# Norms as one power of a sum: means, signs and scales folded into factors, epsilon added on another engine

## The chip, the cores and the metric

The kernel runs on one core of a Trainium2 chip, as one launch. The metric is the device time of that launch in microseconds (us); smaller is better. The engines are called PE (TensorE matmul; its weight loads are listed apart as PEld), DVE (VectorE), ACT (ScalarE), POOL (GpSimd) and SP (SyncE, which here issues DMAs).

## What is computed

Two layers of a decoder, 256 positions, width 1024, all float32. Each layer normalises x, projects it through one combined matrix, runs three groups of attention heads (MoBA with one block of 256, which at this length is plain causal attention; differential attention; DSA, which keeps the 64 keys that an indexer scores highest), projects their outputs back and adds a SwiGLU feed-forward layer.

```python
def rms_norm(x, g):
    y = x * rsqrt(mean(x * x, axis=-1, keepdims=True) + EPS)     # EPS = 1e-6
    return y * g
for l in range(2):
    h = rms_norm(x, attn_norm_g[l])
    (mq, mk, mv, dq, dk, dv, sq, sk, sv, iq, ik, iw) = split(h @ w_in[l])
    def qk(t, nh, g):                       # heads of 64
        return apply_rope(rms_norm(split_heads(t, nh), g), cos, sin)
    moba = attention(qk(mq, 4, qg[0]), qk(mk, 4, kg[0]), mv)
    dq_h, dk_h = qk(dq, 8, qg[1]), qk(dk, 8, kg[1])
    lam = exp(sum(lp[0] * lp[1])) - exp(sum(lp[2] * lp[3])) + lam_init
    diff = (softmax(q1 k1) - lam * softmax(q2 k2)) @ dv
    diff = rms_norm(diff, diff_subln_g[l]) * (1.0 - lam_init)
    score = sum_h(iw * relu(rope(iq) . rope(ik)))      # -inf above the diagonal
    keep  = the min(256, S / 4) keys of highest score
    dsa  = attention(qk(sq, 4, qg[2]), qk(sk, 4, kg[2]), sv, keep)
    x = x + concat(moba, diff, dsa) @ w_out[l]
    h2 = rms_norm(x, ffn_norm_g[l])
    x = x + (silu(h2 @ w_gate[l]) * (h2 @ w_up[l])) @ w_down[l]
```

## The kernel before

**Products.** Every product with a weight matrix is taken in three matmuls that add up in one bank (L618, L619, L620): the weight's rounded part `wh` times the activation's rounded part `hH`, the weight's rest `wl` times `hH`, and `wh` times the activation's rest `hL`. For each loaded weight `raw`, ACT writes `wh` as a copy (L252) and DVE writes `wl` as a subtraction (L541). The positions are two tiles of 128 (`t` = 0, 1). The layer's first part is called the mixers here: the projection in eight chunks of columns, `idx` (the indexer), `sv_iq`, `mqk`, `dq`, `dk`, `sqk`, `mv`, `dv`, with the heads' work in between, then the output projection.

**Who sets the order.** All work is written as Python threads that hand pieces to a planner (`Timeline`). A piece is `V`, `A`, `G` or `T` (DVE, ACT, POOL, PE) with an estimated cost, and a thread can wait for an event or for a buffer. The planner keeps an estimated clock for each engine, takes the piece that can start first, and issues instructions in that order; on the chip each engine then works strictly in that order. So a changed cost or a piece moved to another engine reorders the program around it. DMAs of weights are issued from SP's queue in the order of the loads; `SMALL_FIRST` says ahead of which load the small ones go: the rope angles, the gains of queries and keys (`gqk`), the causal penalties (`pens`, 256 KB), and others.

**The norms.** A reciprocal root is taken on POOL by `rsqrt_mean` (L621): one `tensor_scalar` that multiplies the sum of squares by 1/n and adds epsilon (L626), then a power of -0.5 (L629). There are three kinds.

- Over the width of 1024 (`rx_thread`, L723): ACT squares two halves of a row (L714), POOL adds the two sums (L726), and `rsqrt_mean` gives `rx`. Ahead of the mixers POOL then works out an epsilon for the heads' norms (L733, L735), since the heads are normed from projections that were not scaled by `rx`.
- Over the 64 numbers of a head (`head_rstd`, L806): ACT squares a 128x512 tile (L819), DVE sums it by heads (L823), and `rsqrt_mean` gives eight factors for each position: `dkr` for the keys of the differential heads, `rq` for the others, the queries among them. Another POOL instruction (L833) multiplies the factors of queries by -(64^-0.5). In `qk_thread` (L851) DVE multiplies the roped keys by their factors (L879; in some places ACT does, L871), PE transposes them (L636), and the scores' matmuls (L1037) follow. The queries' factors go into the softmax as a scale for each position (L1007).
- Over the 128 numbers of a differential output head (`diff_out`, L1160): ACT sums squares (L1183), `rsqrt_mean`, DVE multiplies (L1192), PE transposes (L636), and DVE multiplies by the gain (L1204).

**Tables.** `table_thread` (L1377) multiplies the rope angles by the gains of queries and keys, 12 POOL instructions in each layer (L1386, L1391), into the table `tb` that the rope of the next heads reads (L778, L790). `gcol_thread` (L1314) transposes the gains of the width's norms into columns. `lambda_thread` (L1339) loads 256 KB into a work buffer `w` (L1346) and works out lambda on DVE (L1359, L1370). The indexer's scores are picked by rounds of MAX (L986) and MATCH_REPLACE (L987), then turned into penalties (L991, L994).

## Time and profile before

| | |
|---|---|
| median of 3 runs | 650.46 us (648.71 to 650.91) |
| the profiled execution | 650.43 us, of which the span from first to last instruction is 648.4 us |
| PE busy | 633.2 us, 98% of the span |
| DVE busy | 554.8 us, 86% |
| ACT busy | 411.7 us, 63% |
| POOL busy | 84.2 us, 13% |
| granted TensorE clock | 0.999 of full speed on average |

The shares are means over unlike stages. The projections and feed-forward products keep PE full; in the mixers, and above all in the first 90 us, DVE has as little spare time as PE, and POOL's short norms lie between DVE and PE. The 2.0 us between the execution's time and its span lie outside of every engine's work.

### The profile page before, as it was taken

How to read it: one execution, taken by the hardware profiler on the slowest of the kernel's cores; microseconds unless marked ns; L12 is line 12 of the kernel's file. 1: busy time of each engine (PE TensorE's matmuls, PEld its weight loads, DVE VectorE, ACT ScalarE, POOL GpSimd, SP SyncE). 2: the span in 40 equal slices, each digit the busy share in tenths (PEclk: the TensorE clock that was granted, in tenths of full speed). 3: DMA queues.
4: the chain of work that ended last, by engine and by line, in shares of the span. 5: the costliest groups of instructions: out<-in, count | busy, mean ns of one | idle time of the engine just before them, and what ended most of it. 6: DMA issues, size and time to landing. Idle time of an engine off the chain costs nothing.

```text
span 648.4 us, 8749 instructions
## 1 busy us (share of the span) xinstructions
PE 633.2 (98%) x3132; PEld 515.5 (79%) x3132; DVE 554.8 (86%) x924; ACT 411.7 (63%) x733; POOL 84.2 (13%) x119
## 2 busy tenths in 40 slices
PE   9899999999999999999999999999999999999997
PEld 8777877787788888787889788887777888888886
DVE  5789999566999999999488999995599999999861
ACT  6487779647647566556545688894677385565640
POOL 2414340200000000180020333200100000000000
PEclk9999999999999999999999999999999999999999
DMA  8898343607558467328736145343475566670621
GB/s 246 284 307 220 111 151 127 199 2 265 188 183 271 142 187 253 132 66 286 246 122 213 60 131 195 130 151 110 145 245 167 188 230 195 192 252 11 215 110 65
DMA packets 74350, 113.36 MB, mean 175 GB/s; under 512 B 2722, under 2 KB 54724, under 8 KB 74308
## 3 DMA queue, kind: packets, MB, share of 16 engines
q1 hardware_dynamic: 73700, 110.71, 52.5%
q0 software_dynamic: 576, 2.10, 1.8%
q8 instruction: 24, 0.39, 0.3%
q14 instruction: 18, 0.15, 0.1%
q10 hardware_dynamic: 32, 0.01, 0.0%
HBM read 109.66 MB, written 1.05 MB: 171 GB/s over the span
## 4 chain that ended last, share of the span: by engine, by line
PE 70%; DVE 18%; DMA 5%; ACT 4%; issue 1%; POOL 1%; SPq 0%; DVEq 0%; POOLq 0%; ACTq 0%
PE bank L618 21%; PE bank L620 21%; PE bank L619 21%; DVE wl L541 7%; PE bank L636 4%; DMA raw<-in_w_in_dram 2%; DMA raw<-in_w_up_dram 2%; PE bank L1037 1%; DMA w<-in_diff_lambda_dram 1%; ACT p L1018 1%; ACT wh L252 1%; DVE qr L550 1%; DVE tb L976 1%; DVE tb L987 1%; ACT p L254 1%
## 5 line engine op out<-in xcount | busy, mean ns | idle before, releaser
L252 ACT ACTIVATE wh<-raw 128x1024 fp32r<-128x1024 f32 (+4 forms) x205 | 207.7, 1039 | 99.6 <-PE bank L620 48.3
L541 DVE TENSOR_TENSOR wl<-raw,wh 128x1024 fp32r<-128x1024 f32 (+4 forms) x205 | 245.4, 1206 | 24.6 <-ACT wh L252 23.9
L618 PE MATMUL bank<-wh,hH 128*128 128x512 f32 (+3 forms) x488 | 191.4, 392 | 2.5 <-ACT hH L252 2.3
L619 PE MATMUL bank<-wl,hH 128*128 128x512 f32 (+3 forms) x488 | 185.3, 380 | 2.0 <-DVE wl L541 1.9
L620 PE MATMUL bank<-wh,hL 128*128 128x512 f32 (+3 forms) x488 | 185.4, 380 | 0.7 <-DVE hL L668 0.5
L618 PEld LDWEIGHTS bank<-wh,hH 128*128 128x128 f32 x488 | 91.9, 188 | 22.6 <-issue 4.5
L620 PEld LDWEIGHTS bank<-wh,hL 128*128 128x128 f32 x488 | 91.8, 188 | 18.3 <-DVE hL L668 2.0
L619 PEld LDWEIGHTS bank<-wl,hH 128*128 128x128 f32 x488 | 92.0, 189 | 17.9 <-DVE wl L541 3.5
L618 PE MATMUL bank<-wh,qk 128*128 128x512 f32 x176 | 70.3, 400 | 0.0
L620 PE MATMUL bank<-wh,qk 128*128 128x512 f32 x176 | 69.7, 396 | 0.6 <-DVE qk L1246 0.6
L619 PE MATMUL bank<-wl,qk 128*128 128x512 f32 x176 | 69.6, 395 | 0.0
L252 ACT ACTIVATE qk<-bank 128x512 fp32r<-128x512 f32 (+4 forms) x54 | 26.1, 501 | 29.7 <-PE bank L636 29.0
L620 PEld LDWEIGHTS bank<-wh,qk 128*128 128x128 f32 x176 | 33.2, 189 | 9.2 <-DVE qk L1246 1.5
L618 PEld LDWEIGHTS bank<-wh,qk 128*128 128x128 f32 x176 | 33.2, 188 | 7.6 <-ACT qk L252 0.4
L619 PEld LDWEIGHTS bank<-wl,qk 128*128 128x128 f32 x176 | 33.2, 189 | 7.4
L618 PE MATMUL bank<-wh,pv 128*128 128x512 f32 x96 | 38.0, 395 | 0.0
L619 PE MATMUL bank<-wl,pv 128*128 128x512 f32 x96 | 37.9, 395 | 0.0
L620 PE MATMUL bank<-wh,pv 128*128 128x512 f32 x96 | 37.9, 395 | 0.0
L1018 ACT ACTIVATE p<-p,small 128x128 f32<-128x128 f32 (+1 forms) x64 | 28.6, 451 | 3.7 <-DVE small L1007 3.6
L757 DVE TENSOR_TENSOR x<-x,bank 128x512 f32<-128x512 f32 x16 | 11.0, 686 | 22.0 <-PE bank L620 22.0
L618 PE MATMUL bank<-wh,mH 128*128 128x512 f32 x64 | 26.1, 407 | 0.0
L636 PE MATMUL bank<-ident,p 128*128 128x128 f32 x160 | 25.0, 275 | 0.9 <-DVE p L1226 0.6
(147 smaller groups left out, 905.1 us busy)
## 6 DMA issues: line engine op xcount, KB each, us to landing
raw<-in_w_in_dram SPq DMA_DIRECT2D x22, 1024.0 KB, 5.2
raw<-in_w_down_dram SPq DMA_DIRECT2D x22, 1024.0 KB, 5.0
raw<-in_w_gate_dram SPq DMA_DIRECT2D x32, 512.0 KB, 4.1
raw<-in_w_up_dram SPq DMA_DIRECT2D x32, 512.0 KB, 5.0
raw<-in_w_out_dram SPq DMA_DIRECT2D x8, 1024.0 KB, 4.8
raw<-in_w_in_dram SPq DMA_DIRECT2D x4, 768.0 KB, 7.0
wl<-raw POOLq DMA_DIRECT2D x4, 512.0 KB, 7.1
tb<-in_w_gate_dram SPq DMA_DIRECT2D x4, 512.0 KB, 5.5
```

The lines of the kernel that those rows point to most:

```text
L252: nc.scalar.activation(dst, src, AF.Copy)
L254: nc.scalar.activation(dst, src, AF.Copy, scale=scale)
L541: lambda: nc.vector.tensor_sub(lo[:, cs], raw[:, cs], h[:, cs].bitcast(F32)),
L550: return V(n, lambda: nc.vector.tensor_tensor(dst, a, b, op=op))
L618: nc.tensor.matmul(o, aH[:, kt, tok], wH[:, k, cols], start=start, stop=False)
L619: nc.tensor.matmul(o, aH[:, kt, tok], wL[:, k, cols], start=False, stop=False)
L620: nc.tensor.matmul(o, aL[:, kt, tok], wH[:, k, cols], start=False, stop=stop)
L636: nc.tensor.transpose(o, i, ident)
L757: e = yield V(512, lambda: nc.vector.tensor_add(xt[t][:, cs], xt[t][:, cs], bank))
L976: lambda: nc.vector.scalar_tensor_tensor(sc, rl[:, i * n : (i + 1) * n], iws[t][:, h : h + 1], prev, op0=OP.mult, op1=OP.add,),
L987: end = yield V(n, lambda: nc.vector.match_replace(sc, m8, sc, NEG_IDX))
L1018: lambda: nc.scalar.activation(p[:, spans[t]], p[:, spans[t]], AF.Exp, bias=mn[:, t : t + 1], scale=-1.0, accum_out=se[t],),
```

## The change

The factors of the norms are redefined so that a reciprocal root is one POOL instruction, the power of a sum.

- `rsqrt_mean` becomes `rsqrt`: the power alone, without the multiplication by 1/n. What is missing is put elsewhere: the width's gains `gcol` are multiplied by the root of 1024 as they are copied (DVE), the gains of the differential outputs by a root of 128/1024 more, the keys' gains by the root of 64, and the queries' gains by -1, once, on POOL ahead of layer 0's tables.
- The queries' factors are then right without L833. Since their sign moves, the penalties in `pens` that the indexer uses are multiplied by -1 (POOL, once), and the indexer's own by a sign in L991.
- Epsilon is added by itself. For the width, POOL adds it to the first half's sum of squares as soon as that is there. For the heads DVE adds it (the new L827, `small<-small,ss 128x8`), 16 times in the kernel. For the differential outputs POOL adds it, in the place of L626.
- The heads' epsilon takes one POOL instruction in place of two.
- `pens` is loaded ahead of one more weight, and the tables wait for it.

```diff
-SMALL_FIRST = {5: "ropes", 6: "gqk", 8: "pens", 10: "late"}
+SMALL_FIRST = {5: "ropes", 6: "gqk", 7: "pens", 10: "late"}
...
-    def rsqrt_mean(dst, ssum, n, inv, eps=EPS):
-
-        yield G(170, lambda: nc.gpsimd.tensor_scalar(dst, ssum, inv, eps, op0=OP.mult, op1=OP.add))
-        return (
-            yield G(
-                290 + 166 * n, lambda: nc.gpsimd.tensor_tensor(dst, dst, nhalf[:, :n], op=OP.pow)
-            )
+    def rsqrt(dst, src, n):
+
+        return G(
+            290 + 166 * n, lambda: nc.gpsimd.tensor_tensor(dst, src, nhalf[:, :n], op=OP.pow)
         )
...
-        yield ("wait", both)
         s = ss2[t]
+        yield ("wait", halves[0])
+        yield G(170, lambda: nc.gpsimd.tensor_scalar_add(s[:, 0:1], s[:, 0:1], D * EPS))
+        yield ("wait", halves[1])
         yield G(170, lambda: nc.gpsimd.tensor_add(s[:, 0:1], s[:, 0:1], s[:, 1:2]))
-        e = yield from rsqrt_mean(rx[t], s[:, 0:1], 1, 1.0 / D)
+        e = yield rsqrt(rx[t], s[:, 0:1], 1)
         ready.done(e)
         if mixers:
 
-            yield G(
+            e = yield G(
                 170,
-                lambda: nc.gpsimd.tensor_scalar(s[:, 1:2], s[:, 0:1], 1.0 / D, EPS, op0=OP.mult, op1=OP.add),
+                lambda: nc.gpsimd.tensor_scalar_mul(s[:, 1:2], s[:, 0:1], HD * EPS),
             )
-            e = yield G(170, lambda: nc.gpsimd.tensor_scalar_mul(s[:, 1:2], s[:, 1:2], EPS))
...
         yield ("wait", eps_ready[t])
-        e = yield from rsqrt_mean(dst, small[:, :n], n, 1.0 / HD, ss2[t][:, 1:2])
+        yield V(
+            n, lambda: nc.vector.tensor_scalar_add(small[:, :n], small[:, :n], ss2[t][:, 1:2]), ap=1
+        )
+        e = yield rsqrt(dst, small[:, :n], n)
         SMALL.put(small, e)
         done["rstd"].done(e)
-        nq = done["queries"]
-        if nq:
-            e = yield G(
-                200, lambda: nc.gpsimd.tensor_scalar_mul(dst[:, :nq], dst[:, :nq], -(HD ** -0.5))
-            )
-        done["all"].done(e)
...
-            lambda: nc.vector.tensor_scalar(sc, sc, -1.0e38, NEG, op0=OP.is_gt, op1=OP.mult),
+            lambda: nc.vector.tensor_scalar(sc, sc, -1.0e38, -NEG, op0=OP.is_gt, op1=OP.mult),
...
-        yield from rsqrt_mean(ro[:, :4], ro[:, :4], 4, 1.0 / P)
+        yield G(170, lambda: nc.gpsimd.tensor_scalar_add(ro[:, :4], ro[:, :4], P * EPS))
+        yield rsqrt(ro[:, :4], ro[:, :4], 4)
...
-        e = yield V(n, lambda: nc.vector.tensor_copy(gcol[:, c0 : c0 + n], bank[:, :n]))
+        e = yield V(
+            n, lambda: nc.vector.tensor_scalar_mul(gcol[:, c0 : c0 + n], bank[:, :n], D ** 0.5)
+        )
...
-                        gcol[:, c : c + 1], gcol[:, c : c + 1], 1.0 - lam_init(l)
+                        gcol[:, c : c + 1], gcol[:, c : c + 1],
+                        (1.0 - lam_init(l)) * (P / D) ** 0.5,
...
         yield ("wait", small_in["ropes"])
+        yield ("wait", small_in["pens"])
         yield ("wait", small_in["gqk"])
+        if l == 0:
+
+            for s, factor in enumerate((-1.0, HD ** 0.5)):
+                yield G(500, lambda: nc.gpsimd.tensor_scalar_mul(gqk[:, s], gqk[:, s], factor))
+            yield G(
+                300, lambda: nc.gpsimd.tensor_scalar_mul(pens[:, 0, P:], pens[:, 0, P:], -1.0)
+            )
```

Counted over the program, POOL loses 30 rows (115 to 85), DVE gains 17 (852 to 869: 16 are the new adds; three more of the copies that make `wh` also fall to DVE instead of ACT), and PE and SP keep theirs, in another order. The lines of the changed file are a few lower than before's for the same statement (L879 is L874 there, L823 is L822, L636 is L633).

On DVE, in the mixers of layer 0 where the keys of the differential heads (chunk `dk`) are normed, the rows of before are these; `small_129` and `small_130` are the sums of squares of the two tiles, `dkr_85_162` the factors.

```order
L823 TENSOR_REDUCE small_129<-w_26_101 128x8
L778 TENSOR_TENSOR qr_105<-bank_67,tb_159 128x512
L823 TENSOR_REDUCE small_130<-w_28_103 128x8
L790 TENSOR_TENSOR w_29_104<-bank_67,tb_159 128x512
L541 TENSOR_TENSOR wl_100<-raw_90,wh_99 128x1024
L550 TENSOR_TENSOR qr_105<-qr_105,w_29_104 128x512
L541 TENSOR_TENSOR wl_100<-raw_90,wh_99 128x1024
L987 MATCH_REPLACE tb_159<-small_118,tb_159 128x256
L879 TENSOR_TENSOR qr_105<-qr_105,dkr_85_162 128x512
```

The same place of the changed kernel, from the rope's product behind the first sum on (L822 stands in front of it):

```order
L777 TENSOR_TENSOR qr_105<-bank_69,tb_159 128x512
L827 TENSOR_SCALAR small_129<-small_129,ss_71_146 128x8
L789 TENSOR_TENSOR w_26_101<-bank_69,tb_159 128x512
L822 TENSOR_REDUCE small_130<-w_28_103 128x8
L541 TENSOR_TENSOR wl_100<-raw_90,wh_99 128x1024
L550 TENSOR_TENSOR qr_105<-qr_105,w_26_101 128x512
L541 TENSOR_TENSOR wl_100<-raw_90,wh_99 128x1024
L827 TENSOR_SCALAR small_130<-small_130,ss_72_147 128x8
L541 TENSOR_TENSOR wl_94<-raw_91,wh_93 128x1024
L777 TENSOR_TENSOR qr_106<-bank_68,tb_159 128x512
L822 TENSOR_REDUCE small_131<-w_27_102 128x8
L874 TENSOR_TENSOR qr_105<-qr_105,dkr_85_162 128x512
```

The second tile's sum now passes through an add that stands behind two weight subtractions and a rope's addition, and the multiply of the keys behind one more subtraction, a rope's product and a sum.

On PE, where the second tile's keys of chunk `mqk` are transposed in layer 0 (`qr_107`), before has the four transposes behind the last of four trios of matmuls into one bank:

```order
L618 MATMUL bank_67<-wh_97,hH_139 128x512
L619 MATMUL bank_67<-wl_98,hH_139 128x512
L620 MATMUL bank_67<-wh_97,hL_140 128x512
L636 MATMUL bank_64<-ident_73,qr_107 128x128 x4
L618 MATMUL bank_68<-wh_97,hH_139 128x512
```

The changed kernel has them behind the first of the four (the bank is `bank_65` there):

```order
L620 MATMUL bank_66<-wh_95,hL_140 128x512
L618 MATMUL bank_65<-wh_97,hH_139 128x512
L619 MATMUL bank_65<-wl_98,hH_139 128x512
L620 MATMUL bank_65<-wh_97,hL_140 128x512
L633 MATMUL bank_69<-ident_73,qr_107 128x128 x4
```

They stand three trios, nine matmuls, earlier among the products.

On SP's queue, early in the program, the penalties move ahead of one load of a weight and lambda's input behind two (`raw` are weights, `w_28_103` receives lambda's input):

```order
 L350 DMA raw_90<-in_w_in_dram 128x4x384
+L1296 DMA pens_83<-in_causal_dram 128x2x256
 L350 DMA raw_91<-in_w_in_dram 128x4x512
-L1300 DMA pens_83<-in_causal_dram 128x2x256
 L350 DMA raw_92<-in_w_in_dram 128x4x512
```

```order
 L350 DMA raw_92<-in_w_in_dram 128x4x512
-L1346 DMA w_28_103<-in_diff_lambda_dram 128x512
 L350 DMA raw_90<-in_w_in_dram 128x4x512
 L350 DMA raw_91<-in_w_in_dram 128x4x512
+L1345 DMA w_28_103<-in_diff_lambda_dram 128x512
```

The rows with - are before's, those with + the changed kernel's: the penalties are issued one weight earlier, lambda's input two weights later.

## Rows read from the trace of the kernel before

**Rows 1.** The page: busy time of each engine; the chain that ended last.

```profile
PE 633.2 (98%) x3132; PEld 515.5 (79%) x3132; DVE 554.8 (86%) x924; ACT 411.7 (63%) x733; POOL 84.2 (13%) x119
...
PE 70%; DVE 18%; DMA 5%; ACT 4%; issue 1%; POOL 1%; SPq 0%; DVEq 0%; POOLq 0%; ACTq 0%
```

**Rows 2.** Windows, two stretches of the mixers (us, then busy us of each engine).

```profile
56.00:85.00 29.00, 27.68 (x141) 22.21 (x141) 27.77 (x79) 21.06 (x52) 11.15 (x10) 1.00 0.52 158
...
365.00:396.00 31.00, 31.00 (x162) 25.26 (x162) 30.80 (x81) 23.91 (x53) 11.77 (x13) 1.00 0.33 104
```

**Rows 3.** Timeline from 73 us, around layer 0's `dk` keys (start, us, engine).

```profile
78.48 1.67 POOL L629 TENSOR_TENSOR dkr<-dkr,nhalf 128x8 f32<-128x8 f32 x1
...
78.55 0.67 DVE L823 TENSOR_REDUCE small<-w 128x8 f32<-128x512 f32 x1
...
79.73 1.21 DVE L541 TENSOR_TENSOR wl<-raw,wh 128x1024 fp32r<-128x1024 f32 x1
...
80.25 1.35 POOL L626 TENSOR_SCALAR dkr<-small,ss 128x8 f32<-128x8 f32 x1
...
81.47 1.22 DVE L541 TENSOR_TENSOR wl<-raw,wh 128x1024 fp32r<-128x1024 f32 x1
...
81.69 2.49 POOL L629 TENSOR_TENSOR dkr<-dkr,nhalf 128x8 f32<-128x8 f32 x1
...
84.21 0.69 DVE L879 TENSOR_TENSOR qr<-qr,dkr 128x512 f32<-128x512 f32 x1 [1.13 <-POOL dkr L629]
...
84.96 1.09 PE L636 MATMUL bank<-ident,qr 128*128 128x128 f32 x8 [1.32 <-DVE qr L879]
```

**Rows 4.** Timeline from 54 us, the second tile's `mqk` keys in layer 0.

```profile
55.35 0.39 PE L620 MATMUL bank<-wh,hL 128*128 128x512 f32 x1
...
55.49 0.40 DVE L879 TENSOR_TENSOR qr<-qr,rq 128x256 f32<-128x256 f32 x1
55.58 0.80 PE L636 MATMUL bank<-ident,qr 128*128 128x128 f32 x4
```

**Rows 5.** Instructions by line and shape on DVE (busy us, mean ns, idle before).

```profile
L541 DVE TENSOR_TENSOR wl<-raw,wh 128x1024 fp32r<-128x1024 f32 x194 | 236.0, 1225 | 24.3 <-ACT wh L252 23.8
...
L1143 DVE TENSOR_SCALAR small<-small,nlam 128x2 f32<-128x2 f32 x8 | 1.8, 222 | 0.0
...
L896 DVE TENSOR_SCALAR iw<-bank,rx 128x8 f32<-128x8 f32 x4 | 1.1, 279 | 1.0 <-PE bank L620 1.0
```

**Rows 6.** Timeline, DVE alone, 86 to 106 us: two penalty instructions.

```profile
86.35 0.28 DVE L991 TENSOR_SCALAR tb<-tb 128x256 f32<-128x256 f32 x1
...
95.18 0.41 DVE L994 TENSOR_TENSOR tb<-tb,pens 128x256 f32<-128x256 f32 x1
```

**Rows 7.** Instructions by line, DVE, 273.4 to 288.6 us (POOL at layer 1's tables).

```profile
L541 DVE TENSOR_TENSOR wl<-raw,wh 128x1024 fp32r<-128x1024 f32 x4 | 5.8, 1462 | 0.0
```

**Rows 8.** Waits of DVE, 24 to 60 us (us in total, times, longest).

```profile
DVE wl L541 <- ACT wh L252: 2.4, 2, 1.7
```

**Rows 9.** Timeline, SP alone, 15 to 48 us: issues of penalties and weights.

```profile
15.55 1.27 SPq L1300 DMA_DIRECT2D pens<-in_causal_dram  x1
...
37.36 3.49 SPq L350 DMA_DIRECT2D raw<-in_w_in_dram  x2
```

**Rows 10.** DMA issues, 10 to 48 us: the penalties (KB, us to landing).

```profile
pens<-in_causal_dram SPq DMA_DIRECT2D x1, 256.0 KB, 11.1
```

**Rows 11.** Chain of waits, 30 to 48 us, around lambda (start, us, what).

```profile
34.66 6.44 DMA w<-in_diff_lambda_dram
```

**Rows 12.** Timeline, DVE alone, 40 to 48 us: lambda's first, the table's first reader.

```profile
41.12 0.23 DVE L1359 CUSTOM_DVE_ANT_0 w<-w 128x64 f32<-128x64 f32 x1 [0.67 <-DMA w<-in_diff_lambda_dram]
...
44.06 0.69 DVE L778 TENSOR_TENSOR qr<-bank,tb 128x512 f32<-128x512 f32 x1
```

**Rows 13.** Waits of PE, 114 to 150 us: the end of layer 0's mixers.

```profile
PE bank L636 <- DVE qr L1192: 1.0, 2, 0.7
```

**Rows 14.** Timeline, POOL alone, 146 to 151 us: the second norm.

```profile
146.75 0.19 POOL L726 TENSOR_TENSOR ss<-ss 128x1 f32<-128x1 f32 x1 [8.44 <-ACT w L714]
147.03 0.19 POOL L626 TENSOR_SCALAR rx<-ss 128x1 f32<-128x1 f32 x1
```

More of the change, by code (lines that the diff above doesn't have):

```diff
@@ L721, in square_thread, with rx_thread @@
         both.done(e)
-    def rx_thread(t, both, ready, mixers):
-        yield ("wait", both)
+    def rx_thread(t, halves, ready, mixers):
         s = ss2[t]
+        yield ("wait", halves[0])
+        yield G(170, lambda: nc.gpsimd.tensor_scalar_add(s[:, 0:1], s[:, 0:1], D * EPS))
+        yield ("wait", halves[1])
         yield G(170, lambda: nc.gpsimd.tensor_add(s[:, 0:1], s[:, 0:1], s[:, 1:2]))
-        e = yield from rsqrt_mean(rx[t], s[:, 0:1], 1, 1.0 / D)
+        e = yield rsqrt(rx[t], s[:, 0:1], 1)
         ready.done(e)
         if mixers:
-            yield G(
+            e = yield G(
                 170,
-                lambda: nc.gpsimd.tensor_scalar(s[:, 1:2], s[:, 0:1], 1.0 / D, EPS, op0=OP.mult, op1=OP.add),
+                lambda: nc.gpsimd.tensor_scalar_mul(s[:, 1:2], s[:, 0:1], HD * EPS),
             )
-            e = yield G(170, lambda: nc.gpsimd.tensor_scalar_mul(s[:, 1:2], s[:, 1:2], EPS))
             eps_ready[t].done(e)
@@ L744, in norm @@
         for t in range(NT):
-            both = Event(2)
+            halves = [Event(), Event()]
             for hf in range(2):
@@ L748, in norm @@
                 tl.spawn(norm_thread(t, hf, g0, h_ready[t][hf], r, kept), 0)
-                tl.spawn(square_thread(t, hf, None if kept else h_ready[t][hf], both), 1)
-            tl.spawn(rx_thread(t, both, r_ready[t], not kept), 1)
+                tl.spawn(square_thread(t, hf, None if kept else h_ready[t][hf], halves[hf]), 1)
+            tl.spawn(rx_thread(t, halves, r_ready[t], not kept), 1)
         return h_ready, r_ready
@@ L854, in qk_thread @@
         b = heads(bank)
-        nq = sum(p[1] for p in parts if not p[3])
-        ev = {"read": Event(), "rstd": Event(), "all": Event(), "queries": nq}
+        ev = {"read": Event(), "rstd": Event()}
         tl.spawn(head_rstd(bank, b, 8, t, rstd, ev), 10, full.time)
@@ L884, in qk_thread @@
         done.done(own.time)
-        yield ("wait", ev["all"])
-        r_done.done(ev["all"].time)
+        yield ("wait", ev["rstd"])
+        r_done.done(ev["rstd"].time)
     def idx_thread(t, bank, full, r_ready, done):
```

## The prediction

> **What bounds the kernel now.** The page comes first: PE is busy 633.2 of 648.4 us, and the chain that ended last runs through PE for 70% of the span, through DVE for 18% and through POOL for 1% [rows 1]. So nearly all of the time is products that the change leaves alone, and the change can act only where PE waits for an operand that passes through a norm. The windows tell where that is. In layer 0's mixers from 56 to 85 us PE is busy 27.68 of 29.00 us and DVE 27.77, so both are nearly full and PE's idle time is 1.3 us; in the like stretch of layer 1 PE is busy 31.00 of 31.00 [rows 2]. In layer 1 nothing can be won there, and only DVE's lateness could show.
>
> The 1.3 us is one wait, and the timeline shows its chain [rows 3]. DVE ends the second tile's sum of squares behind 78.55; POOL, still in the first tile's power, takes the epsilon at 80.25 (1.35 us, beside DVE's work) and the power at 81.69 (2.49 us); DVE's multiply of the keys starts at 84.21 after 1.13 us of waiting, and PE's eight transposes at 84.96 after 1.32 us. Two more waits of this kind, 1.0 us in all, stand at the end of layer 0's mixers behind the differential norm [rows 13]. POOL's short steps are on the path there, and in the second norm of the width, where L626 adds 147.03 - 146.75 = 0.28 us by the step from start to start [rows 14].
>
> **The change part by part.** I follow how late PE comes, against before, at the places where it waits or would wait; lateness at two places in a row is not added, since the later wait swallows the earlier.
>
> *The price of an add on DVE.* Before has no `small<-small,ss`. The nearest rows are a 128x2 `TENSOR_SCALAR` of 0.222 us and a 128x8 one that reads a bank, 0.279 us [rows 5]. Rows of DVE overlap a little: L823 and L790 are 0.67 to 0.68 us each, and from L823's start to the next L541 pass 79.73 - 78.55 = 1.18 us [rows 3], so a step is some 0.08 us shorter than its row. I take 0.2 us, bounds 0.14 and 0.28; 16 of them are 3.2 us of DVE in both layers, and what counts is how many stand ahead of a multiply that PE waits for.
>
> *`mqk`, second tile, layer 0.* PE's transposes there start at 55.58, when the multiply of 55.49 has nearly ended [rows 4]: no time to spare. The order puts them nine matmuls earlier. Matmuls follow each other by 55.58 - 55.35 = 0.23 us, so PE asks 2.1 us earlier, at about 53.5. DVE's work ahead of the multiply is hardly changed (two adds more, one round of the indexer's picking less), so the operand comes at the same time as before, and PE waits about 2.1 us. This is new lateness of 2.1, and the work that was to cover it comes behind.
>
> *`dk`, layer 0.* Before, DVE was free for the multiply at 84.21 - 1.13 = 83.08. Ahead of it the changed order has, in addition, one subtraction (1.22), one product and one sum of a head's tile (0.67 each) [rows 3], six adds (1.2), and the two penalty instructions of the second tile that were behind it (0.28 and 0.41) [rows 6]; with 0.08 off for each of the five long ones this is 2.3 + 1.2 + 0.5 = 4.0 us. DVE gets there at 87.1. POOL's side is ready before: the second sum ends some 2.5 us later than 79.1 (five adds, a product, a picking step, the penalties), the second add follows behind three rows that took 79.73 to about 82.6 (2.9 us), and the power takes 1.67 as its undisturbed row does [rows 3]: 81.6 + 2.9 + 0.2 + 1.7 = 86.4. So the power leaves the path, and DVE's own queue takes its place. The transposes start at about 87.8 instead of 84.96. But they now stand behind six matmuls (1.4) and the other tile's four transposes (half of 1.09) [rows 3], 1.8 to 1.9 us of work that before came later. PE is late by 87.8 - 84.96 - 1.8 = 1.0 us. The 2.1 us from `mqk` less the 1.32 that before waited here is 0.8. Both ways say about +1.0.
>
> *Tables and penalties.* The 12 table instructions of layer 0 and three new scalings wait for `pens`, because POOL works in order. Issued at 15.55 and landing 11.1 us later [rows 9, 10], it came at 26.7; one load earlier, some 26. The tables then run until about 34, where before DVE was working alone, well ahead of the first reader at 44.06 [rows 12]. What it costs DVE is shown by layer 1, where the same 12 run beside a full DVE: subtractions take 1.462 us there [rows 7] against a mean of 1.225 [rows 5], 0.24 each, and eight of them are 1.9 us. From 24 to 41 us DVE had 2.4 us of waiting for ACT [rows 8], which takes part of it. I take +0.5, bounds 0 and 2.0.
>
> POOL loses as well: the epsilon of 1.35 and the power of 2.49 ran beside two subtractions, the power of 1.67 did not [rows 3]. The Trainium skill ("SBUF — State Buffer", section "SBUF: two separate sides") says that GpSimd and a VectorE instruction with two inputs in SBUF share a port pair as an exclusive lock, so that the loser fully blocks. The trace agrees that both get longer; a loss of 0.24 us on a subtraction is less than a whole table instruction. If DVE lost every lock it would make the third rival below.
>
> *Lambda.* Its load moves behind two weights whose issues end at 37.36 + 3.49 = 40.85 [rows 9]. It took 6.44 us [rows 11], so it lands at 47.3. DVE waited 0.67 us for it at 41.12 [rows 12]; in the new order its first reader stands behind twelve of the indexer's sums, a picking round and a rope's product. Between 41.12 and 44.06 [rows 12] DVE did seven such sums beside lambda's own small steps, so 0.4 us each, and I put the reader at about 46.5 (an estimate). One wait of 0.7 takes the place of another: 0, bounds 0 and 2.
>
> So PE comes 1.0 + 0.5 = 1.5 us late out of the keys (bounds 0 and 4).
>
> *End of layer 0's mixers.* The 1.0 us of waits remains if the differential norm is late by as much as PE, and goes if not. POOL's two steps stay two there. I take -0.5, bounds -1.0 and 0.
>
> *Second norms.* Epsilon goes in while ACT still squares the other half, so L626 leaves both chains: 2 x 0.28 = -0.55 [rows 14].
>
> *Layer 1.* Eight adds, 1.6 us of DVE, with PE's operands ready in time before [rows 2] and DVE at 30.80 of 31.00, so no cover beyond a fraction. The order moves PE's rows as well, and the loads of the first layer's feed-forward part give DVE back its lateness. I take +0.4, bounds 0 and 2.
>
> The scaled copy of `gcol` replaces a copy of the same size and the dropped L833 stood behind the power, where only the softmax reads it: 0.
>
> Sum: 1.5 - 0.5 - 0.55 + 0.4 = +0.85 us on the profiled execution of 650.43, which is the runs' median of 650.46 within 0.03. **651.3 us.**
>
> **The rivals.** 0.3% of this time, about what a measurement can tell from no change, is 1.95 us: 648.5 to 652.4 is the same.
>
> - *The chain gets shorter (faster).* If the planner's new order suits the chip, the multiply is not kept back by DVE's queue, the wait of 1.32 goes with POOL's epsilon, the 1.0 at the end of the mixers goes and the norms give 0.55: 650.4 - 2.9 = 647.6. For it speaks that POOL's 1.35 is on the path [rows 3]; against it, DVE is full there and gets more work [rows 2]. It needs the new `mqk` wait below 1.3 us, or it is eaten. Chance 0.2.
> - *Layer 1 turns from PE to DVE (slower).* There PE and DVE are full at once. If the `dk` multiply of layer 1 stands as far behind as that of layer 0, PE waits there 2 to 2.5 us for the first time: 653.5. It decides once DVE's lateness passes the fraction of a us that PE has in hand. Chance 0.17.
> - *DVE pays for the tables (slower).* If each of the 15 POOL instructions stops DVE for 0.3 us or more, or `pens` comes so late that the first reader waits, DVE is late by 3 to 4 us ahead of `mqk`, and nothing takes it back: 654.5. The 0.24 us a subtraction [rows 7] speaks against more than 2. Chance 0.13.
>
> **How the numbers follow.** The first forecast has the rest, 0.5, with a range of its own from 649.5 to 653.2. For 8 in 10 the range reaches half-way into the rivals on both sides: 648.0 to 654.7. Faster than 648.5 takes the first rival and a little of the forecast: 0.22. Slower than 652.4 takes the two slow rivals and the upper tail of the forecast: 0.36. The same: 0.42.
>
> **What the changed profile would show.** Right: a wait of PE for `mqk`'s second multiply of 1.5 to 2.5 us near 54 us; the `dk` multiply in layer 0 not waiting for POOL but starting as DVE's row before it ends; the L827 rows near 0.2 us; the tables beside a busy DVE between 26 and 35 us; 0.28 us less between the two halves' sum and the power in the second norms. Wrong: no wait at `mqk`, or waits of PE in layer 1's mixers beyond 1 us, or a DVE wait for lambda over 1.5 us, which would undo the sum at that term.

## The result and the profile after

The changed kernel takes 653.56 us (median of 6 runs, 652.61 to 654.72) against 649.66 of before (6 runs): ratio 1.0074, 95% interval 1.0061 to 1.0086. By the ratio it is slower by some 4.8 us, by the two medians by 3.9. That is inside the range of the forecast, but on the side to which it had given a chance of 0.36, and 2.3 us above the number it gave.

The profiled executions differ by less: 652.61 us with a span of 650.5, against 650.43 with 648.4. Before's profiled execution was among its slower ones: in it a weight came late, and PE waited 1.0 us for `wl` at 26 us, where experiments 6 and 12 below, whose program is the same up to there, show 0.2 and 0.8. The changed kernel's was its fastest of six. So the traces tell where time went, and the sizes are taken from timed runs.

The page of the changed kernel, first its busy times, then the chain that ended last; they answer to [rows 1].

```profile
PE 634.4 (98%) x3132; PEld 515.2 (79%) x3132; DVE 561.4 (86%) x943; ACT 409.0 (63%) x730; POOL 85.1 (13%) x90
...
PE 82%; DVE 9%; DMA 4%; POOL 1%; ACT 1%; issue 1%; SPq 1%; DVEq 0%; POOLq 0%; ACTq 0%
```

PE's share of the chain went from 70% to 82%, and DVE's from 18% to 9%. DVE is busy 6.6 us more. By the two pages DVE has 19 instructions more (924 to 943: the 16 adds and three copies) and POOL 29 fewer (119 to 90); the 17 and 30 given with the change do not fit these rows. The windows answer to [rows 2]; the first row is a stretch that the forecast did not look at for PE. Of it, here is before, then experiment 6, whose program is before's in this stretch (columns: window, its us, then busy us and instructions of PE, PEld, DVE, ACT, POOL, granted clock, DMA share, GB/s):

```profile
24.00:41.00 17.00, 15.30 (x90) 12.05 (x89) 15.06 (x26) 13.31 (x22) 0.92 (x3) 1.00 0.83 262
...
24.00:41.00 17.00, 15.85 (x92) 12.73 (x93) 15.84 (x37) 13.49 (x22) 2.56 (x5) 1.00 0.93 300
```

and the changed kernel, with the two stretches of [rows 2]:

```profile
24.00:41.00 17.00, 13.74 (x84) 11.10 (x83) 16.93 (x29) 11.85 (x19) 9.52 (x12) 1.00 0.84 274
56.00:85.00 29.00, 28.88 (x146) 23.00 (x145) 28.90 (x89) 20.20 (x49) 5.87 (x5) 1.00 0.58 161
365.00:396.00 31.00, 31.00 (x160) 25.30 (x159) 30.80 (x86) 24.66 (x54) 7.64 (x5) 1.00 0.32 103
```

From 56 to 85 us PE lost 0.1 us instead of 1.3: the wait at the differential keys is gone. From 24 to 41 us it is busy 13.74 us instead of 15.30 in before and 15.85 in experiment 6: it is idle for 3.3 us instead of 1.7 or 1.2. DVE, which had 1.9 us to spare there (1.2 in experiment 6), has none. What PE waited for in the whole span (total us, times, longest):

```profile
PE bank L619 <- DVE wl L541: 3.2, 3, 1.4
PE bank L633 <- DVE qr L902: 2.1, 2, 1.3
...
PE bank L633 <- DVE qr L550: 1.1, 1, 1.1
PE bank L633 <- ACT w L254: 0.9, 2, 0.4
...
PE bank L633 <- DVE qr L874: 0.5, 1, 0.5
...
PE bank L618 <- ACT hH L252: 0.3, 1, 0.3
PE bank L633 <- DVE qr L1188: 0.2, 1, 0.2
```

The waits for L902 and L550 are 3.2 us in three places; before had one of 0.5 us there, and experiment 6 one of 0.9. They are the transposes of the indexer's queries and keys:

```profile
27.30 0.33 PE L633 MATMUL bank<-ident,qr 128*128 128x128 f32 x1 [1.34 <-DVE qr L902]
...
31.36 0.33 PE L633 MATMUL bank<-ident,qr 128*128 128x128 f32 x1 [0.80 <-DVE qr L902]
...
33.33 0.33 PE L633 MATMUL bank<-ident,qr 128*128 128x128 f32 x1 [1.12 <-DVE qr L550]
```

At the same time the tables run, behind the penalties:

```profile
22.67 0.53 POOL L1386 TENSOR_SCALAR pens<-pens 128x128 f32<-128x128 f32 x1 [1.35 <-DMA pens<-in_causal_dram]
23.16 1.59 POOL L1393 TENSOR_TENSOR tb<-gqk,ropes 128x192 f32<-128x192 f32 x1
...
28.45 2.80 POOL L1398 TENSOR_TENSOR tb<-gqk,ropes 128x96 f32<-128x96 f32 x2
...
31.76 1.76 POOL L1398 TENSOR_TENSOR tb<-gqk,ropes 128x96 f32<-128x96 f32 x2
```

The penalties were in at 22.6, not at 26 as forecast; the tables ran from 23.2 to 33.5, where the forecast had their end at 34, and two pairs of L1398 took 2.80 and 1.76 us. DVE's five whole subtractions (128x1024) in that time averaged 1.343 us:

```profile
L541 DVE TENSOR_TENSOR wl<-raw,wh 128x1024 fp32r<-128x1024 f32 x5 | 6.7, 1343 | 0.0
```

At the `dk` keys of layer 0, which answer to [rows 3], the queue went nearly as the forecast worked it out (start, us, engine):

```profile
84.50 0.23 DVE L827 TENSOR_SCALAR small<-small,ss 128x8 f32<-128x8 f32 x1
...
84.63 1.22 DVE L541 TENSOR_TENSOR wl<-raw,wh 128x1024 fp32r<-128x1024 f32 x1
...
84.80 2.54 POOL L627 TENSOR_TENSOR dkr<-small,nhalf 128x8 f32<-128x8 f32 x1 [2.56 <-DVE small L827]
...
87.38 0.69 DVE L874 TENSOR_TENSOR qr<-qr,dkr 128x512 f32<-128x512 f32 x1 [0.34 <-POOL dkr L627]
...
88.13 0.66 PE L633 MATMUL bank<-ident,qr 128*128 128x128 f32 x4
```

The multiply starts at 87.38 (forecast 87.1), the transposes at 88.13 (87.8), and PE does not wait. DVE itself was there 0.34 us earlier; the power, which a subtraction overtook by 0.17 us, took 2.54 us instead of the 1.67 put down, so it stayed on the path that it was to leave. The add costs about what it was priced at: 0.223 us in the mean of its 16 rows, where 0.2 was taken.

### The profile page after: what moved, and what is told of

Read it like the earlier page. It is cut to its first block, busy times and chain, and to the rows that moved or that the text cites. A ratio compares the mean times of both kernels' runs of the same rounds, so it can differ in the third digit from the quotient of the medians.

```text
span 650.5 us, 8740 instructions
## 1 busy us (share of the span) xinstructions
PE 634.4 (98%) x3132; PEld 515.2 (79%) x3132; DVE 561.4 (86%) x943; ACT 409.0 (63%) x730; POOL 85.1 (13%) x90
## 4 chain that ended last, share of the span: by engine, by line
PE 82%; DVE 9%; DMA 4%; POOL 1%; ACT 1%; issue 1%; SPq 1%; DVEq 0%; POOLq 0%; ACTq 0%
PE bank L618 25%; PE bank L620 25%; PE bank L619 25%; PE bank L633 4%; DVE wl L541 3%; DMA raw<-in_w_up_dram 2%; PE bank L1032 2%; DMA w<-in_diff_lambda_dram 1%; DMA x<-in_x_dram 1%; PE bank L1102 1%; DVE mL L550 1%; DVE qr L550 1%; POOL rx L627 0%; PE bank L949 0%; POOL small L627 0%
## 5 line engine op out<-in xcount | busy, mean ns | idle before, releaser
L252 ACT ACTIVATE wh<-raw 128x1024 fp32r<-128x1024 f32 (+4 forms) x202 | 203.9, 1038 | 92.7 <-PE bank L620 41.9
L620 PEld LDWEIGHTS bank<-wh,hL 128*128 128x128 f32 x488 | 91.7, 188 | 18.4 <-DVE hL L665 2.1
L627 POOL TENSOR_TENSOR rq<-small,nhalf 128x8 f32<-128x8 f32 x12 | 21.8, 1814 | 67.4 <-DVE small L827 67.4
L1393 POOL TENSOR_TENSOR tb<-gqk,ropes 128x192 f32<-128x192 f32 x8 | 10.0, 1245 | 123.9 <-DVE wl L541 123.9
```

Source lines behind the costliest of these rows:

```text
L252: nc.scalar.activation(dst, src, AF.Copy)
L620: nc.tensor.matmul(o, aL[:, kt, tok], wH[:, k, cols], start=False, stop=stop)
L627: 290 + 166 * n, lambda: nc.gpsimd.tensor_tensor(dst, src, nhalf[:, :n], op=OP.pow)
L1393: yield G(550, lambda: nc.gpsimd.tensor_tensor(cur["rc"][:, t, js, :], gl[:, s], cc, op=OP.mult))
```

## The experiments

They were timed on two chips, 5 to 8 on one and the others on the other, each beside the kernel before (medians 648.8 to 649.0 us, 647.6 to 651.6 over the runs); a ratio is to the runs of before on the same chip. Where an experiment keeps an order, the planner is told the costs of the kernel whose order is wanted, and the instructions of the other are put out at those places.

**1. The change's instructions in before's order.** In before's file each piece keeps its planned cost, and puts out the changed instruction, or nothing (excerpt; the remark behind # is not in the code):

```diff
-        yield G(170, lambda: nc.gpsimd.tensor_scalar(dst, ssum, inv, eps, op0=OP.mult, op1=OP.add))
+        yield G(170, add)      # heads: the add on nc.vector; width: nothing; diff: the add on nc.gpsimd
...
-            e = yield G(
-                200, lambda: nc.gpsimd.tensor_scalar_mul(dst[:, :nq], dst[:, :nq], -(HD ** -0.5))
-            )
+            e = yield G(200, lambda: None)
```

> All of the change's instructions (16 adds on DVE, one power on POOL, folded factors, scalings ahead of the tables), but the planner is told before's costs, so PE, ACT, DVE and SP keep before's order, with the adds as rows that stand in between. If the order is what costs (the first theory), the time is that of before or up to 1 us less, since the two second norms and the wait of 1.3 us at the differential keys get shorter: ratio 0.998 to 1.001. If the instructions cost (the rival: adds on a full DVE, tables beside it), it stands near the changed kernel: 1.005 to 1.008.

Measured: ratio 1.0065 (1.0046 to 1.0085). The order theory alone falls: the instructions cost some 4 us in an order that was not changed. PE waits 3.9 us for multiplies of keys, three times, where before had 1.3 once.

**2. Before's instructions in the change's order.** The reverse, in the changed file:

```diff
         yield V(
             n,
-            lambda: nc.vector.tensor_scalar_add(small[:, :n], small[:, :n], ss2[t][:, 1:2]), ap=1
+            lambda: nc.gpsimd.tensor_scalar(
+                dst, small[:, :n], 1.0 / HD, ss2[t][:, 1:2], op0=OP.mult, op1=OP.add
+            ),
+            ap=1,
         )
```

> The reverse: before's instructions (POOL multiplies and adds epsilon, scales the queries' factors, no add on DVE) in the order that the planner makes of the change's costs, the earlier load of the penalties with it. First theory (order): as slow as the changed kernel or slower by up to 1 us, ratio 1.005 to 1.010. Rival (instructions): as before, 0.999 to 1.002.

Measured: 1.0036 (1.0022 to 1.0049), between the bands of the two theories. Half of the loss comes with the order alone, without one instruction of the change. Its trace has two of the waits at the indexer's transposes, with no scaling and with tables that start nearly as early as before's (18.6 us against 18.4) and end at 26.9 (against 24.9):

```profile
27.36 0.33 PE L637 MATMUL bank<-ident,qr 128*128 128x128 f32 x1 [1.26 <-DVE qr L915]
...
32.22 0.33 PE L637 MATMUL bank<-ident,qr 128*128 128x128 f32 x1 [0.88 <-DVE qr L550]
```

**3. Only the earlier load of the penalties.** `SMALL_FIRST = {5: "ropes", 6: "gqk", 7: "pens", 10: "late"}` in the kernel before.

> The kernel before with the one number changed that loads the penalties one weight earlier; about six rows move on PE. If the load itself costs, up to 1 us is added, ratio up to 1.002; if only the wider order costs, 0.999 to 1.001.

Measured: 1.0002 (0.9990 to 1.0014). No cost of the load can be told.

**4. Another order, for no reason.** `1.1 * ns + 150.0` becomes `1.1 * ns + 140.0` in the planner's cost of a POOL piece of the kernel before.

> The kernel before with the planner's fixed cost of a POOL instruction set 10 ns lower: every instruction is the same, about a hundred rows of PE and ACT move. If a new order alone is worth microseconds (first theory), the time moves by 1 to 4 us, up or down: ratio below 0.9985 or above 1.0015. If orders that the planner makes are worth the same, 0.999 to 1.001.

Measured: 1.0013 (1.0001 to 1.0025), between the two bands, so it decides for neither. This order is worth some 0.8 us, a third of what the change's order costs; that the change's order costs because of where it puts particular rows is what experiment 2's trace suggests, not what this run shows.

**5. The first experiment with the heads' add on POOL.** `nc.vector.tensor_scalar_add` becomes `nc.gpsimd.tensor_scalar_add`.

> As the first run (the change's instructions in before's order), but the heads' epsilon is added by POOL instead of DVE; everything else of the change stays, the scalings ahead of the tables too. In that first run layer 1's differential keys had a power of 4.28 us on POOL instead of 1.6 to 1.7, beside three DVE instructions with two inputs, and PE waited 1.7 us there. If the add on DVE is what costs in before's order (first theory: it delays the power into DVE's next instructions), the time falls back to before, ratio 0.998 to 1.002. If the tables and scalings cost (rival), it stays near 1.006.

Measured: 1.0014 (1.0003 to 1.0025). Back to before, but for a remainder of the size of experiment 7's. In before's order the add on DVE is most of the loss.

**6. Only the heads' epsilon on DVE.** The kernel before with one engine changed:

```diff
-        e = yield from rsqrt_mean(dst, small[:, :n], n, 1.0 / HD, ss2[t][:, 1:2])
+        e = yield from rsqrt_mean(dst, small[:, :n], n, 1.0 / HD, ss2[t][:, 1:2], nc.vector)
```

> The kernel before, in its own order, with one thing changed: the heads' multiply and epsilon (L626, 16 of them) run on DVE instead of POOL. Nothing is folded. First theory: most of the first run's loss, ratio 1.004 to 1.007, with a wait of PE of 1.5 us or more at layer 1's differential keys. Rival (tables and scalings): 0.999 to 1.002.

Measured: 1.0056 (1.0043 to 1.0069). Nearly all of the first experiment's loss. Its profiled execution was its fastest, 650.75 us against a median of 652.60, so the trace holds only about half of that loss. Its timeline at the differential keys of layer 1:

```profile
389.76 0.22 DVE L627 TENSOR_SCALAR dkr<-small,ss 128x8 f32<-128x8 f32 x1
389.89 1.22 DVE L541 TENSOR_TENSOR wl<-raw,wh 128x1024 fp32r<-128x1024 f32 x1
...
390.06 4.30 POOL L630 TENSOR_TENSOR dkr<-dkr,nhalf 128x8 f32<-128x8 f32 x1 [5.40 <-DVE dkr L627]
...
391.02 0.69 DVE L550 TENSOR_TENSOR qr<-qr,w 128x512 f32<-128x512 f32 x1
...
391.62 1.22 DVE L541 TENSOR_TENSOR wl<-raw,wh 128x1024 fp32r<-128x1024 f32 x1
...
394.40 0.69 DVE L880 TENSOR_TENSOR qr<-qr,dkr 128x512 f32<-128x512 f32 x1 [1.55 <-POOL dkr L630]
...
395.14 0.66 PE L637 MATMUL bank<-ident,qr 128*128 128x128 f32 x4 [1.71 <-DVE qr L880]
```

The power starts 0.17 us after a subtraction and lasts 4.30 us, through that subtraction, the rope's addition and the second subtraction, all with two inputs in SBUF; these end at 392.8, and about a power of its usual length later, at 394.4, the multiply can start. PE, which never waited in this stretch of before, waits 1.71 us. In before the power was ahead of the same subtraction by 0.05 us, and both took their usual time:

```profile
391.59 1.67 POOL L629 TENSOR_TENSOR dkr<-dkr,nhalf 128x8 f32<-128x8 f32 x1
...
391.64 1.22 DVE L541 TENSOR_TENSOR wl<-raw,wh 128x1024 fp32r<-128x1024 f32 x1
```

The Trainium skill ("SBUF — State Buffer", section "SBUF: two separate sides") says that of a GpSimd instruction that reads SBUF and a VectorE instruction with two inputs in SBUF the one that starts first holds the shared port pair for the whole instruction, and the other blocks. The trace agrees for POOL as the loser (4.30 us against 1.67; with one such subtraction ahead instead of three rows, at layer 0's `dk` keys, 2.49 in before and 2.54 in the changed kernel). It does not for DVE as the loser: the subtraction that started 0.05 us behind a power took 1.22 us as always, so a power does not keep DVE out for its whole length. An add on DVE ahead of a power gives DVE's next row the start, since that row is already waiting on DVE's own queue.

A start ahead by 0.05 us is no safe margin, though. In experiment 2, where POOL adds the epsilon, the power at the same keys started 0.06 us ahead of the same subtraction and lasted 4.54 us:

```profile
391.52 4.54 POOL L628 TENSOR_TENSOR dkr<-dkr,nhalf 128x8 f32<-128x8 f32 x1
...
391.58 1.22 DVE L541 TENSOR_TENSOR wl<-raw,wh 128x1024 fp32r<-128x1024 f32 x1
```

In experiment 5 a power 0.02 us ahead took 2.75 us. So where the two starts are this close, the traces do not bear out that the first to start wins, and a power can be held off without any add on DVE; PE did not wait for either of these two. Over all the traces here, each 128x8 power that started while a DVE row with two inputs in SBUF was running took longer than usual (64 powers, 1.74 to 4.30 us), and of 130 that started ahead of the next such row by 0.08 us or more all but two took 1.64 to 1.68 us (the two, right behind a DMA issue of POOL's, 2.0); of 18 that were ahead by less, three were held off.

**7. Only the three scalings.** The gains and the penalties are multiplied by 1.0 in the kernel before, so nothing else differs:

```diff
+        if l == 0:
+            for k in range(2):
+                nc.gpsimd.tensor_scalar_mul(gqk[:, k], gqk[:, k], 1.0)
...
         nc.sync.dma_start(pens, causal.rearrange("s p k -> p s k"))
+        nc.gpsimd.tensor_scalar_mul(pens[:, 0, P:], pens[:, 0, P:], 1.0)
```

> The kernel before with three more POOL instructions and nothing taken away: the queries' and keys' gains and the penalties are multiplied by 1.0 where the change scales them, so the tables start later and their second half waits for the penalties. First theory: 0.999 to 1.002, since DVE has spare time there. Rival: 1.003 or more, with a longer wait of PE for the indexer's transposes between 24 and 34 us.

Measured: 1.0015 (1.0006 to 1.0024), 1.0 us. Small, but not nothing, and of the size of the remainder of experiment 5. The traces do not place it: from 24 to 41 us PE is idle for 1.8 us here, but for 1.0 in experiment 5, which has the scalings too, and for 1.2 in experiment 6, which has none.

**8. The changed kernel once more**, unchanged, for a second profile.

> The changed kernel once more, for a second profile: its other timed runs had a mean granted clock of 0.997, the profiled one 1.0. If a stretch at the lower clock is part of its loss, the windows of this profile show one after a wait of PE, near the indexer's transposes; the span is then 651 to 652.5 us. Otherwise the span is again 650.5.

Measured: span 649.4 us at a clock of 1.0, one run of 651.41 us. No stretch at the lower clock in this one, and the span is below both that were expected; it decides nothing about the others.

**9. The changed kernel, timed here**, unchanged.

> The changed kernel itself, timed on the chip of the other runs. If its loss is that of the new order and the scalings (0.36% and 0.15% by the runs before), the ratio is 1.004 to 1.006 at a clock of 1.0; if the adds on DVE cost in its own order what they cost in before's, 1.008 or more.

Measured: 1.0070 (1.0054 to 1.0087), between the two expectations, and not at a clock of 1.0: the runs show 0.996 to 0.999. The two at 0.999 took 652.2 and 652.5 us (0.52% above before, as the first expectation had it), the four at 0.996 or 0.997 took 653.0 to 654.4, 1.6 us more in the mean. This profile (span 652.1, clock 0.997) shows where. The same three waits of PE as above:

```profile
27.23 0.33 PE L633 MATMUL bank<-ident,qr 128*128 128x128 f32 x1 [1.37 <-DVE qr L902]
...
31.27 0.33 PE L633 MATMUL bank<-ident,qr 128*128 128x128 f32 x1 [0.77 <-DVE qr L902]
...
33.61 0.33 PE L633 MATMUL bank<-ident,qr 128*128 128x128 f32 x1 [1.48 <-DVE qr L550]
```

and the windows of two us behind them (the third number from the right is the granted clock):

```profile
30.00:32.00 2.00, 1.23 (x8) 0.79 (x6) 2.00 (x5) 1.33 (x3) 2.00 (x3) 1.00 0.23 86
32.00:34.00 2.00, 0.52 (x3) 0.27 (x2) 2.00 (x3) 1.63 (x5) 1.80 (x3) 1.00 0.95 259
34.00:36.00 2.00, 2.00 (x7) 1.58 (x7) 2.00 (x8) 1.67 (x3) 0.00 (x0) 0.65 0.71 270
36.00:38.00 2.00, 2.00 (x7) 1.50 (x6) 2.00 (x2) 0.00 (x0) 0.00 (x0) 0.50 0.93 262
38.00:40.00 2.00, 2.00 (x23) 1.56 (x24) 0.73 (x2) 1.97 (x3) 0.00 (x0) 1.00 1.02 322
```

PE was idle for 2.25 of the four us from 30 to 34. In the two windows after that the granted clock is 0.65 and 0.50, which is the level of 1.2 GHz instead of 2.4 for most of 34 to 38 us, and from 38 us it is back. PE is called busy all the while, with 7 instructions in a window. That is (1 - 0.65) x 2 + (1 - 0.50) x 2 = 1.7 us of full speed lost. In the first profile and in that of experiment 8, with waits within 0.4 us of these, the clock stayed at 1.0. For the other runs below 1.0 there is no trace; that their clock fell at the same place is not shown.

**10. Epsilon as a 65th square.** A version of my own in before's order, to need neither L626 nor an add for the heads (excerpt; the remark behind # is not in the code):

```diff
-            e = yield A(n * HD, lambda: nc.scalar.activation(sq, b, AF.Square), bank=bank)
+            def emit():      # sq is now (p, h, d) over columns d * 8 + h, with d = 64 for epsilon
+                eps = ss2[t][:, 1:2].to_broadcast([P, 8])
+                nc.scalar.activation(wide[:, 512:], eps, AF.Copy)
+                nc.scalar.activation(sq[:, :, :HD], b, AF.Square, scale=HD ** -0.5)
+
+            e = yield A(n * HD, emit, bank=bank)
```

> A version of my own, in before's order: ACT squares with a scale, so that the sums are means; epsilon is put as a 65th column beside each head's 64 squares (a 128x8 copy on ACT ahead of the square, 16 times) and DVE's sum takes it in, so the heads need neither L626 nor an add on DVE; the width's epsilon is added in the instruction that adds the two halves. POOL loses 24 instructions, DVE gains none. If POOL's early start ahead of DVE's two-input instructions is what matters, the power starts 0.4 us earlier, always ahead of them, the wait at layer 0's differential keys gets shorter: ratio 0.997 to 0.999. If strided squares or ACT's copies cost, 1.001 or more.

Measured: 1.0088 (1.0071 to 1.0105), the slowest of all. One group shows the most of it (instructions by line and shape):

```profile
L832 DVE TENSOR_REDUCE small<-w 128x8 f32<-128x520 f32 x16 | 18.6, 1160 | 0.4 <-ACT w L826 0.4
```

The sum over a stride of eight numbers takes 1.160 us, where [rows 3] have 0.67 for the sum over neighbours: 16 x 0.49 = 7.8 us more of DVE. ACT pays as well: its square writes with the same stride and takes 1.168 us, 0.595 in before. How the 5.6 us of loss divide between the two is open. It says nothing of the idea, only of this layout.

**11. The changed kernel with the heads' add on POOL**, and the planner told so: `yield V(n, ...tensor_scalar_add)` becomes `yield G(170, ...)` on `nc.gpsimd`.

> The changed kernel with the heads' epsilon added by POOL in place of DVE, and the planner told so, which gives a third order. If the DVE add is the loss also in the planner's own order, 0.999 to 1.002; if new orders and the scalings cost, 1.003 to 1.006.

Measured: 1.0043 (1.0026 to 1.0060), as the second theory expected. Most of the changed kernel's loss stays without the add on DVE. Its trace has the same three waits for L902 and L550 from 24 to 41 us, 3.3 us, and its runs clocks from 0.994 to 1.0. Three runs at 0.999 or 1.0 took 650.5 to 651.2 us, three at 0.994 to 0.997 took 651.7 to 653.2. At either level that is 1.5 us below experiment 9 in the mean, so the gain without the add on DVE is not one of the clock; it comes with another order, and with few runs.

**12. Experiment 6 with the epsilon directly behind the sum.** The DVE row is put out with L823 instead of one rope's product later.

> As the run with the heads' multiply and epsilon on DVE in before's order, with one thing changed: each of these stands directly behind its sum instead of one rope product later, so that the power starts while DVE reads a bank, ahead of the subtractions with two inputs. If POOL's power is held off by DVE's two-input instructions that start first, the power at layer 1's differential keys is 1.7 us again, PE's wait of 1.7 us there goes, and the ratio falls to 0.999 to 1.002. If the work that DVE does more of is the cost, or the handing over, it stays at 1.004 or more.

Measured: 1.0043 (1.0029 to 1.0057). The mechanism is as expected at its place:

```profile
391.81 1.66 POOL L630 TENSOR_TENSOR dkr<-dkr,nhalf 128x8 f32<-128x8 f32 x1 [4.94 <-DVE dkr L824]
...
392.23 1.22 DVE L541 TENSOR_TENSOR wl<-raw,wh 128x1024 fp32r<-128x1024 f32 x1
...
395.84 0.66 PE L637 MATMUL bank<-ident,qr 128*128 128x128 f32 x4 [0.24 <-DVE qr L883]
```

The power now starts 0.42 us ahead of the subtraction, takes 1.66 us, and PE waits 0.24 us instead of 1.71. But the total fell by 0.13% only, less than was expected, and the intervals of 6 and 12 overlap. So being held off is not shown to cost time in the whole; what remains, 0.43% (0.29 to 0.57), is not settled. What is left for it is DVE's work itself, 16 rows of 0.22 us on a queue that has little to spare: the trace shows four waits of PE for L883, 2.4 us in all, where before has one of 1.3. That this is the cause is argued, not shown.

## Why the prediction was right or wrong

**The bound and the places.** That PE's waits decide was right. That the change can act only where PE waits for an operand that passes through a norm was not: it moves rows of all engines, and its largest waits are at the indexer's transposes from 25 to 34 us, which stand behind DVE's queue and not behind a norm's root. The places were chosen from where PE waited before, and here it hardly did. The step that failed is "Tables and penalties": "The tables then run until about 34, where before DVE was working alone, well ahead of the first reader at 44.06 ... I take +0.5". It asked who reads the tables and when, and not who else waits for DVE in that stretch. PE does: by the two timelines the new order puts the indexer's transposes three to nine matmuls earlier among the products. Experiment 2 shows waits of 2.1 us there without the late tables; with them they are 3.2, and the subtractions among DVE's rows take 1.343 us against a mean of 1.225. In place of +0.5 PE is idle for 3.3 us from 24 to 41 us, against 1.7 in before's profiled execution and 1.2 in experiment 6. On top of it comes, in most of the timed runs, a mean clock of 0.996 or 0.997, some 1.6 us by experiment 9, which no term held.

The time rose, as forecast, and stayed inside the range; that is in part luck. The lateness of 2.1 us that the sum had at `mqk` did not come about there, and about as much came at the indexer, where none was foreseen.

**`mqk`.** At the second tile's keys a wait of 2.1 us was forecast; there is none. The rows are the first tile's transposes, then the second tile's, nine matmuls behind them where before had eighteen:

```profile
53.41 0.44 PE L633 MATMUL bank<-ident,qr 128*128 128x128 f32 x2 [0.53 <-DVE qr L874]
...
55.65 0.41 DVE L874 TENSOR_TENSOR qr<-qr,rq 128x256 f32<-128x256 f32 x1
55.75 0.80 PE L633 MATMUL bank<-ident,qr 128*128 128x128 f32 x4
```

The second tile's multiply came at 55.65, against 55.49 in before, as worked out. PE came to it at 55.75 and not at 53.5, because it was late already, and had waited 0.5 us more at the first tile. In experiment 2, with the same order and PE less late, it does wait at the second tile's keys, 1.11 us at 55.71. The forecast's own rule, that a later wait swallows an earlier one, had its first term missing. No wait at this place was one of the forecast's own signs that it was wrong.

**`dk`, layer 0.** Right by size: the add, the multiply and the transposes are within 0.4 us of the working. One step was not right: POOL's power was to leave the path, and the multiply waited 0.34 us for it.

**Lambda.** It landed at 40.46 + 7.0 = 47.5 (forecast 47.3), but DVE was there sooner and waited 1.5 us, not 0.7:

```profile
47.51 0.23 DVE L1358 CUSTOM_DVE_ANT_0 w<-w 128x64 f32<-128x64 f32 x1 [1.54 <-DMA w<-in_diff_lambda_dram]
```

That is within the bounds, but just over the 1.5 us that the forecast had named as a sign that its sum is wrong at this term. PE does not wait for lambda itself; the first tile's multiply of `mqk`, for which it waits 0.53 us, stands behind it on DVE. How much of that is lambda's no run separates.

**End of layer 0's mixers.** The waits for L1192 went from 1.0 to 0.2 us: -0.8 where -0.5 was taken.

**Second norms.** The power now follows the two halves' sum directly, 0.27 us behind its start instead of 0.56, as worked out; but that sum starts later behind ACT's second square, and from the end of that square to the power it is 0.77 us (148.16 to 148.93) against 0.63 in before (146.68 to 147.31):

```profile
148.66 0.19 POOL L726 TENSOR_TENSOR ss<-ss 128x1 f32<-128x1 f32 x1 [2.81 <-ACT w L711]
148.93 0.57 POOL L627 TENSOR_TENSOR rx<-ss,nhalf 128x1 f32<-128x1 f32 x1
```

It gave nothing, and could not: in before the root was not on PE's path there. ACT's scaled x was ready at 147.90 + 1.34 = 149.24, and PE came to its transposes at 150.14 without a wait:

```profile
147.90 1.34 ACT L254 ACTIVATE w<-x,rx 128x512 f32<-128x512 f32 x2 [1.22 <-POOL rx L629]
...
150.14 1.03 PE L636 MATMUL bank<-ident,w 128*128 128x128 f32 x8
```

Before's wait of 1.0 us for `hH` comes only behind these eight transposes. So in experiment 1, which has the shorter norm in before's order, the waits for `hH` stay at 2.3 us in all, as in before. In the changed kernel the order splits the eight, and the waits of 1.0 us are gone in both layers; but some ten us later PE waits 1.35 us for a `wl` (at 161.89, and 1.4 again in layer 1). Two new waits of 0.4 us, one a layer, are for ACT's scaled x (L254): in layer 0 the power of the first tile lasted 1.57 us, beside a subtraction that started 0.10 us ahead, where before's took 0.55. So the term of -0.55 was mis-sized: in before's order it is 0.

**Layer 1.** The rival that PE would wait there for the first time (653.5 us, "2 to 2.5 us" at the `dk` multiply) is what happens in before's order (experiments 1 and 6, 1.7 us). In the change's own order the planner moved PE's rows, and the stretch stays full: 31.00 of 31.00. So this rival's number is near the measured one, but not for its reason.

**The sum.** Of a loss of 0.70%, 0.36% comes with the order and before's instructions, 0.15% with the scalings (timed on the other chip), and up to 0.27% goes when the add leaves DVE (experiments 9 and 11, whose intervals overlap a little, and whose orders differ). These do not add up strictly: the instructions alone cost 0.65% in before's order and the order alone 0.36%, more than the whole together, so each brings a lateness that hides another. The term that was mis-sized most is the one whose stretch was not searched for waits.

No version beat the kernel before. The nearest are the earlier load alone (1.0002), before in another order (1.0013) and the folded factors with the add on POOL in before's order (1.0014).

## What to carry to other kernels

When a planner reorders a program, compare the order of the waiting engine against that of the one it waits for over the whole of the tight part, and not only where waits stood before; a transpose that moves six matmuls ahead while its operand does not come sooner by as much can become a wait, whatever the instruction mix. To tell an order from its instructions, keep the planner's costs and swap what they put out: two runs separate them, though their two losses need not add up to the whole. A short POOL step between two DVE rows should start clearly ahead of DVE's two-input rows; moving the step in front of it onto DVE gives those rows the start. Here that made a step of 1.67 us last 4.30; what it costs the whole kernel stayed within the noise of two experiments.

## What was not expected of the hardware

A power of 1.67 us on POOL lasted 4.30 us when a DVE instruction with two inputs in SBUF had started 0.17 us earlier and two more followed without a gap. When POOL was 0.42 us ahead it kept its length; at 0.01 to 0.07 us ahead it mostly kept it, but lasted 2.75 us in two cases and 4.54 in one.

The granted clock fell to its lower level for most of 34 to 38 us after PE had been idle for three waits of 0.8 to 1.5 us within 8 us, in one profile of three with nearly the same waits.

A DVE sum whose inputs lie eight numbers apart took 1.160 us for 128x520, against 0.67 for 128x512 of neighbours.
